# Delta-rule heads of a hybrid encoder block: decays taken with ScalarE's bias, norms on transposed tiles, two-step doubling levels, and another order of the lanes

## The chip, the cores and the metric

The kernel runs on one core of a Trainium2 chip. The core has five engines that run at the same time and wait for each other by semaphores: TensorE (PE in the profile; its weight loads are PEld), VectorE (DVE), ScalarE (ACT), GpSimd (POOL) and SyncE (SP, which here only issues DMAs). PE writes its results to PSUM, which has eight banks of 128 x 512 fp32 values. The metric is the time of one execution on the device, in microseconds (us); lower is better.

## The reference, cut to what matters

A trunk of two layers works on 512 tokens of width 2048 in fp32. The even layer has neighbourhood attention (6 heads), a gated delta rule in both directions (6 heads) and attention to a memory; the odd layer has differential attention (6 heads) and attention to the memory. The change touches the delta rule of the even layer:

```python
q = l2norm(q) * (HEAD_DIM ** -0.5); k = l2norm(k)
G = jnp.cumsum(g, axis=-1)
decay = jnp.exp(jnp.where(lower_incl, G[..., :, None] - G[..., None, :], -jnp.inf))
a_mat = jnp.where(lower_strict, jnp.einsum('bhnid,bhnjd->bhnij', kb, k) * decay, 0.0)
sol = lax.linalg.triangular_solve(a_mat + jnp.eye(C, dtype=f32), rhs, left_side=True, lower=True)
qk = jnp.einsum('bhnid,bhnjd->bhnij', q, k) * decay
q_dec = q * jnp.exp(G)[..., None]

def step(S, xs):
    u_c, w_c, qk_c, qd_c, kd_c, ge = xs
    v_new = u_c - jnp.einsum('bhcd,bhde->bhce', w_c, S)
    o = jnp.einsum('bhcd,bhde->bhce', qd_c, S) + jnp.einsum('bhij,bhje->bhie', qk_c, v_new)
    S = S * ge[..., None, None] + jnp.einsum('bhcd,bhce->bhde', kd_c, v_new)
    return S, o
```

It runs once forwards and once on the flipped tokens, and the two outputs are added and normed.

## The kernel before

Most of the work is GEMMs against streamed weights. Each fp32 operand is split into a high part that PE can take in one pass (`wh`, `hi`, by an ACT copy) and the rest (`wl`, `lo`, by a DVE subtraction), and each product is the sum of three passes, `hi*wh + hi*wl + lo*wh`. Products of 128 x 128 in the delta rule and all transposes are done in plain fp32.

The order on PE is written by hand. A GEMM is a generator (`chunk`, `group`) that yields after about 350 columns or more, and at each yield `Lanes.step` runs (line 222): it goes over five queues of side work and advances the front task of each by one step, up to that task's next `yield`, if a small clock kept during the build says that what the last step made is ready by now. A step puts its instructions at the end of the queue of each engine that it uses; every engine takes its queue in order. The lanes are: 0 the recurrence (`dn_rec`, and `dn_finish`, which norms the sum of both directions), 1 attention (`na_task`, memory and differential attention), 2 preparation (`dn_prep`), 3 convolution taps (`dn_taps`), 4 the doubling levels (`dn_levels`). When attention's head h+1 is projected (`na_head`), its GEMM of 384 columns holds four PSUM banks, one for each 128 tokens; each delta head in recurrence holds one more (`oacc`). All side work takes what is left: `pb()` (line 291) hands out a bank, and PE's first write into it waits until the last reader of the tile that was there has finished. The build's clock does not know of banks.

For each of the six delta heads `dn_prep` (line 973) does the following, in steps. It loads a row of cumulated gates G, broadcast over 128 partitions, for both directions (`g_d`). It transposes k (`tr4`: four 128 x 128 transposes into one bank), squares the result on ACT, sums on DVE, takes `x^-0.5` on POOL (`rsqrt`), and scales k on DVE straight from that bank (`b.kt`). It transposes v, sums the squares of q by four products with a column of ones, transposes the scaled k back, and makes k k^T and k^T q for four chunks of 128 tokens. Then for each direction it makes the decays: for each chunk DVE subtracts a gate column and takes a maximum or minimum with a mask of +-1e30 (`mx_`, `mn_`), one instruction for 128 x 128, ACT takes the exponential of all 512 columns, and POOL multiplies by k k^T (this is `A`), by k^T q (`qk`) and, for `qd`, exp(G) by q. A goes to DRAM in both directions, comes back as 16 x 16 blocks (`a_d`), DVE solves those with 15 short multiplications and 15 reductions, and the result goes through DRAM again (`x_d`) and is loaded as the start `N` of the inverse.

`dn_levels` (line 1078) doubles the block size three times (16, 32, 64) for each direction: a copy of the needed halves to dense tiles on ACT (`dense`), a product (`pps`), a transpose (`mps`), two evacuations (`Mm` on ACT, `Pm` on DVE, with a mask), a second product (`nps`), and a subtraction into `N` on DVE. Each level has three yields and takes three banks.

After the sixth head come the 16 gate GEMMs (`gates`), which multiply each head's finished output by its gate, and the output projection.

Of the kernel before, what the change touches and what calls it, by code (L numbers as in the profile page):

```python
# [10 lines left out]
AF = mybir.ActivationFunctionType  # L11
# [3 lines left out]
P = 128  # L15
# [196 lines left out]
class Lanes:  # L212
# [8 lines left out]

    def step(self):
        c = self.clock
        for q in self.q:
            if q:
                for e in list(q[0]):
                    if e[1] + LAG > c.t["pe"]:
                        continue
                    c.due = 0.0
                    if next(e[0], None) is None:  # L230
                        q[0].remove(e)
                    e[1] = c.due
                if not q[0]:
                    q.pop(0)
# [17 lines left out]
def tile_hybrid(ctx: ExitStack, tc: tile.TileContext, xT, memT, we, wo, wek, wok, weo, woo, vecs, rows, rpb,  # L252
# [576 lines left out]

    g_d = dram.tile([NH * T], F32, name="g_d")  # L830

    def delta_gates():
        load_ba()
        yield 1
# [31 lines left out]
        vec.tensor_copy(G[:, :, 0:6], gv[:, 0, :, 0:6])  # L866
        vec.tensor_copy(G[:, :, 6:12], gv[:, 1, :, 6:12])
        vec.tensor_tensor(sG, G, lnb, op=ALU.add)
        vec.tensor_tensor(ekd, gv[:, 2], G, op=ALU.subtract)
        act(ege, gv[:, 2], AF.Exp)  # L870
        act(ekd, ekd, AF.Exp)
# [101 lines left out]
    def dn_prep(b):  # L973
# [5 lines left out]
            dma(r, bass.AP(tensor=g_d.tensor, offset=g_d.offset + (d * 6 + b.h) * T, ap=[[0, P], [1, T]]))  # L979
            rows_.append(r)  # L980
        b.q, b.k, b.v = b.qkv
        sq = w2()
        act(sq, b.q, AF.Square)
        kps = tr4(b.k)
        sk = w2()
        act(sk, kps, AF.Square)
        ks = small(4)
        vec.tensor_reduce(ks, v3(sk, 4), AX.X, ALU.add)
        vec.tensor_scalar(ks, ks, EPS, None, op0=ALU.add)
        rk = small(4)  # L990
        rsqrt(rk, ks)
# [3 lines left out]
        vps = tr4(b.v)  # L995
        b.vt = w2()
        copy(b.vt, vps)
        qs = pb()
        for t in range(TT):
            mm(qs[:, t:t + 1], sq[:, t * P:(t + 1) * P], ones[:, 0:1], start=True, stop=True)  # L1000
        rq = small(4)
        vec.tensor_scalar(rq, qs[:, 0:4], EPS, None, op0=ALU.add)
        b.rq = small(4)
        rsqrt(b.rq, rq)
        vec.tensor_scalar(b.rq, b.rq, SCALE, None, op0=ALU.mult)
# [13 lines left out]
        for d in range(2):  # L1019
            hd, n = d * 6 + b.h, "fb"[d]  # L1020
            R = rows_[d]
            A = w2()
            for t in range(TT):
                s = slice(t * P, (t + 1) * P)
                vec.scalar_tensor_tensor(A[:, s], R[:, s], sG[:, t, hd:hd + 1], C("mx_" + n), op0=ALU.subtract,
                                         op1=ALU.max)
            act(A, A, AF.Exp, scale=-1.0)
            pool_e.tensor_tensor(A, A, kk, op=ALU.mult)
            b.a.append(A)
            qk = w2()  # L1030
            for t in range(TT):
                s = slice(t * P, (t + 1) * P)
                vec.scalar_tensor_tensor(qk[:, s], R[:, s], G[:, t, hd:hd + 1], C("mn_" + n), op0=ALU.subtract,
                                         op1=ALU.min)
            act(qk, qk, AF.Exp)
            qd = w2()
            act(qd, R, AF.Exp)
            yield 1
            if d == 0:
                At[0] = A  # L1040
            else:
                aps = tr4(A)
                At[1] = w2()
                copy(At[1], aps)
                yield 1
            dma(rows_ap(ad, d), v3(At[d], 4))
            pool_e.tensor_tensor(qk, qk, kq, op=ALU.mult)
            pool_e.tensor_tensor(qd, qd, b.q, op=ALU.mult)
            b.qk.append(qk)
            b.qd.append(qd)  # L1050
# [27 lines left out]
    def dn_levels(b, d):  # L1078


        while len(b.a) <= d:
            yield 1
        A = b.a[d]

# [4 lines left out]
            copy(o.rearrange("p (k s) -> p k s", s=s), half(a, s, 1))  # L1089
            return o  # L1090

        Ad = []
        at = w2()
        Ad.append(dense(A, 16, at[:, 0:256]))
        yield 1
        Ad.append(dense(A, 32, at[:, 256:512]))
        Ad.append(dense(A, 64, w2()[:, 0:256]))
        while b.inv is None:
            yield 1
        N = b.inv[d]  # L1100
        for li, s in enumerate((16, 32, 64)):
            Nd = dense(N, s, w2()[:, 0:256])
            pps = pb()
            for i in range(2):
                c = slice(i * P, (i + 1) * P)
                mm(pps[:, c], Ad[li][:, c], half(N[:, i * 2 * P:(i + 1) * 2 * P], s, 0), start=True, stop=True)
            yield 1
            mps = pb()
            for i in range(2):
                c = slice(i * P, (i + 1) * P)  # L1110
                transpose(mps[:, c], Nd[:, c])
            Mm = w2()
            copy(Mm[:, 0:256], mps[:, 0:256])
            Pm = w2()
            vec.tensor_tensor(v3(Pm[:, 0:256], 2), v3(pps[:, 0:256], 2),
                              lv[:, li, :].unsqueeze(1).to_broadcast([P, 2, P]), op=ALU.mult)
            yield 1
            nps = pb()
            for i in range(2):
                c = slice(i * P, (i + 1) * P)  # L1120
                mm(nps[:, c], Mm[:, c], Pm[:, c], start=True, stop=True)
            vec.tensor_tensor(half(N, s, 0), half(N, s, 0), nps[:, 0:256].rearrange("p (k s) -> p k s", s=s),
                              op=ALU.subtract)
            yield 1
        b.n[d] = N

    def dn_rec(b, d, hd):
# [456 lines left out]
```

## Time and profile before

| | |
|---|---|
| median of 3 runs | 2004.64 us (2000.44 to 2007.24) |
| the profiled execution | 2001.6 us, of which the span from the first to the last instruction is 1999.8 us |
| busy in the span | PE 98%, PE weight loads 84%, DVE 57%, ACT 39%, POOL 7% |
| granted PE clock, mean | 0.996 of full speed |

The share of PE is of time in which a matmul is on its way; what it waits for, and the clock that it is granted, are in other views. In rows of the trace an instruction stands as line, engine, operation and `out<-in` by the program's tile names without their numbers: `pa` is a PSUM bank, `w` a working tile of 128 x 512, `ct` the constants (an identity, among others, so `pa<-ct,w` on line 335 is a transpose), `s` a small column. Nearly all DVE, ACT and POOL instructions are recorded under the helper's line 207.

### The profile page before, as it was taken

The page shows a single profiled execution, that of the slowest core. Times are in us where ns is not written, and L with a number is a line of the kernel's source. Part 1 is how long each engine was busy: PE and PEld are TensorE (multiplying, and loading weights), DVE is VectorE, ACT ScalarE, POOL GpSimd, SP SyncE. Part 2 cuts the span into 40 slices and gives each one's busy share as a digit, 9 for nine tenths or more (in the row PEclk, how much of TensorE's full clock was granted, in tenths as well). Part 3 has the DMA queues.
Part 4 walks back from the last instruction along what each step waited for, and adds up shares of the span by engine and source line. Part 5 has one row for each costly group of instructions (what it writes and reads, how often), then busy time and mean ns, then how long its engine had stood idle before and what let it go on. Part 6 is the DMA issues. An engine that isn't in the chain of part 4 may idle for free.

```text
span 1999.8 us, 25600 instructions
## 1 busy us (share of the span) xinstructions
PE 1966.4 (98%) x9907; PEld 1684.4 (84%) x9907; DVE 1138.8 (57%) x2150; ACT 774.8 (39%) x1388; POOL 138.2 (7%) x127
## 2 busy tenths in 40 slices
PE   9999999999998999999999999999999999999999
PEld 7988899888888788888888888888888888888887
DVE  6676666757576675656334456566556557435322
ACT  5655344444444434334224343434434333324111
POOL 0100020202020202000000000001001010000000
PEclk9999999999999999999999999999999999999999
DMA  6555433323323233324444423222222323333442
GB/s 217 158 166 168 138 99 102 87 85 87 101 81 98 75 117 112 111 91 128 144 151 128 132 85 95 73 97 74 85 95 74 95 76 114 98 113 122 142 142 90
DMA packets 101050, 222.28 MB, mean 111 GB/s; under 512 B 22288, under 2 KB 36928, under 8 KB 100928
## 3 DMA queue, kind: packets, MB, share of 16 engines
q1 hardware_dynamic: 71232, 207.45, 32.9%
q10 hardware_dynamic: 29696, 13.19, 2.5%
q8 instruction: 78, 1.28, 0.3%
q14 instruction: 44, 0.36, 0.1%
HBM read 199.96 MB, written 20.65 MB: 110 GB/s over the span
## 4 chain that ended last, share of the span: by engine, by line
PE 91%; DVE 3%; issue 2%; ACT 1%; DMA 1%; POOL 1%; ACTq 0%; SPq 0%; POOLq 0%; DVEq 0%
PE pa L265 88%; PE pa L335 4%; DVE w L207 2%; ACT w L207 1%; POOL w L207 1%; DVE wl L207 1%; DMA w<-x_d 1%; POOL s L207 0%; DVE s L207 0%; ACT wh L207 0%; DMA w<-in_xT_dram 0%; DMA w<-in_lvl_dram 0%; DVE vn L207 0%; DVE vb L207 0%; ACTq L342 0%
## 5 line engine op out<-in xcount | busy, mean ns | idle before, releaser
L207 ACT ACTIVATE wh<-wr 128x1024 fp32r<-128x1024 f32 (+3 forms) x333 | 341.8, 1027 | 703.1 <-PE pa L265 551.6
L207 DVE TENSOR_TENSOR wl<-wr,wh 128x1024 fp32r<-128x1024 f32 (+3 forms) x333 | 397.6, 1195 | 362.7 <-ACT wh L207 361.7
L265 PE MATMUL pa<-hi,wh 128*128 128x512 f32 x1312 | 519.0, 396 | 0.0
L265 PE MATMUL pa<-hi,wl 128*128 128x512 f32 x1312 | 511.8, 390 | 0.0
L265 PE MATMUL pa<-lo,wh 128*128 128x512 f32 x1312 | 511.5, 390 | 0.0
L265 PE MATMUL pa<-wh,hi 128*128 128x512 f32 (+2 forms) x1088 | 416.3, 383 | 1.3 <-ACT wh L207 1.3
L265 PE MATMUL pa<-wl,hi 128*128 128x512 f32 (+2 forms) x1088 | 405.9, 373 | 0.4 <-DVE wl L207 0.4
L265 PE MATMUL pa<-wh,lo 128*128 128x512 f32 (+2 forms) x1088 | 405.5, 373 | 0.0
L265 PEld LDWEIGHTS pa<-hi,wl 128*128 128x128 f32 x1312 | 246.6, 188 | 52.2
L265 PEld LDWEIGHTS pa<-lo,wh 128*128 128x128 f32 x1312 | 247.1, 188 | 48.4
L265 PEld LDWEIGHTS pa<-hi,wh 128*128 128x128 f32 x1312 | 247.0, 188 | 48.2
L265 PEld LDWEIGHTS pa<-wh,hi 128*128 128x128 f32 x1088 | 205.9, 189 | 28.4 <-ACT wh L207 2.3
L265 PEld LDWEIGHTS pa<-wh,lo 128*128 128x128 f32 x1088 | 205.6, 189 | 28.0
L265 PEld LDWEIGHTS pa<-wl,hi 128*128 128x128 f32 x1088 | 206.2, 190 | 26.6 <-DVE wl L207 0.7
L207 ACT ACTIVATE w<-pa 128x512 f32<-128x512 f32 (+3 forms) x222 | 111.1, 524 | 177.4 <-PE pa L335 98.5
L207 ACT ACTIVATE w<-w 128x512 f32<-128x512 f32 (+4 forms) x285 | 141.9, 536 | 84.6 <-DVE w L207 64.4
L265 PE MATMUL pa<-w,w 128*128 128x256 f32 (+3 forms) x1128 | 167.7, 293 | 4.6 <-DMA w<-x_d 1.9
L265 PEld LDWEIGHTS pa<-w,w 128*128 128x128 f32 (+1 forms) x1128 | 151.5, 188 | 15.7 <-DVE w L207 3.9
L207 POOL TENSOR_TENSOR s<-s,mhalf 128x1 f32<-128x1 f32 (+3 forms) x58 | 75.3, 1299 | 1200.1 <-DVE s L207 1197.1
L207 DVE TENSOR_TENSOR w<-pa,w 128x512 fp32r<-128x512 f32 (+2 forms) x108 | 71.2, 680 | 137.3 <-PE pa L265 108.1
L207 ACT ACTIVATE w<-pa,s 128x256 f32<-128x256 f32 (+1 forms) x104 | 58.7, 570 | 136.6 <-DVE s L207 102.1
L335 PE MATMUL pa<-ct,w 128*128 128x128 f32 (+1 forms) x640 | 92.2, 273 | 8.8 <-ACT w L207 4.2
(151 smaller groups left out, 1437.0 us busy)
## 6 DMA issues: line engine op xcount, KB each, us to landing
wr<-in_wo_dram SPq DMA_DIRECT2D x112, 512.0 KB, 3.6
wr<-in_we_dram SPq DMA_DIRECT2D x75, 512.0 KB, 3.6
wr<-in_weo_dram SPq DMA_DIRECT2D x32, 512.0 KB, 3.6
wr<-in_woo_dram SPq DMA_DIRECT2D x32, 512.0 KB, 3.5
wr<-in_we_dram SPq DMA_DIRECT2D x40, 384.0 KB, 3.1
w<-in_xT_dram SPq DMA_DIRECT2D x32, 256.0 KB, 4.6
wr<-in_wek_dram SPq DMA_DIRECT2D x16, 512.0 KB, 4.3
wr<-in_wok_dram SPq DMA_DIRECT2D x16, 512.0 KB, 3.8
```

The lines of the kernel that those rows point to most:

```text
L207: return f(*a, **k)
L265: nc.tensor.matmul(o, lhsT, rhs, start=start, stop=stop)
L335: nc.tensor.transpose(o, i, ident if idn is None else idn)
```

## The change

Six edits, all in the build of the side work.

- `Lanes.step` goes over the lanes in the order 0, 2, 3, 4, 1: attention's task steps after the others.
- The norms of k and q: k's squares are summed by ACT itself (`accum_out`), in four instructions of 128 columns instead of one of 512 and a DVE reduction. q is transposed too (`tr4(b.q)`, one more bank) and treated in the same way, and the products of its squares with a column of ones go.
- The decays: DVE takes the maximum and the minimum of the row G and the mask once, over 512 columns; the gate column enters as ACT's bias, so ACT does four exponentials of 128 columns where it did one of 512. A tile `gg` now holds -G for that.
- The products with k k^T and k^T q go from POOL to DVE; the one for `qd` stays on POOL. `dn_prep` has two more yields in each direction.
- `dn_levels` waits for the start of the inverse before it copies anything from A; `pps` and `mps` are halves of one bank and are written in one step, `Mm` and `Pm` lie in one tile, the dense copy of N for the next level is made behind the subtraction, and a level has two yields.
- One DVE instruction for -G, once.

```diff
-        for q in self.q:
+        for q in self.q[:1] + self.q[2:] + self.q[1:2]:
...
+        vec.tensor_scalar(gg, G, -1.0, None, op0=ALU.mult)
+        nG.append(gg)
...
-        sq = w2()
-        act(sq, b.q, AF.Square)
         kps = tr4(b.k)
         sk = w2()
-        act(sk, kps, AF.Square)
         ks = small(4)
-        vec.tensor_reduce(ks, v3(sk, 4), AX.X, ALU.add)
+        for t in range(TT):
+            c = slice(t * P, (t + 1) * P)
+            act(sk[:, c], kps[:, c], AF.Square, accum_out=ks[:, t:t + 1])
...
-        qs = pb()
+        qps = tr4(b.q)
+        rq = small(4)
         for t in range(TT):
-            mm(qs[:, t:t + 1], sq[:, t * P:(t + 1) * P], ones[:, 0:1], start=True, stop=True)
-        rq = small(4)
-        vec.tensor_scalar(rq, qs[:, 0:4], EPS, None, op0=ALU.add)
+            c = slice(t * P, (t + 1) * P)
+            act(sk[:, c], qps[:, c], AF.Square, accum_out=rq[:, t:t + 1])
+        vec.tensor_scalar(rq, rq, EPS, None, op0=ALU.add)
...
-            A = w2()
+            A, qk, qd = w2(), w2(), w2()
+            vec.tensor_tensor(v3(A, 4), v3(R, 4), cm(C("mx_" + n)), op=ALU.max)
+            vec.tensor_tensor(v3(qk, 4), v3(R, 4), cm(C("mn_" + n)), op=ALU.min)
             for t in range(TT):
                 s = slice(t * P, (t + 1) * P)
-                vec.scalar_tensor_tensor(A[:, s], R[:, s], sG[:, t, hd:hd + 1], C("mx_" + n), op0=ALU.subtract,
-                                         op1=ALU.max)
-            act(A, A, AF.Exp, scale=-1.0)
-            pool_e.tensor_tensor(A, A, kk, op=ALU.mult)
+                act(A[:, s], A[:, s], AF.Exp, bias=sG[:, t, hd:hd + 1], scale=-1.0)
+            vec.tensor_tensor(A, A, kk, op=ALU.mult)
             b.a.append(A)
-            qk = w2()
+            yield 1
             for t in range(TT):
                 s = slice(t * P, (t + 1) * P)
-                vec.scalar_tensor_tensor(qk[:, s], R[:, s], G[:, t, hd:hd + 1], C("mn_" + n), op0=ALU.subtract,
-                                         op1=ALU.min)
-            act(qk, qk, AF.Exp)
-            qd = w2()
+                act(qk[:, s], qk[:, s], AF.Exp, bias=nG[0][:, t, hd:hd + 1])
             act(qd, R, AF.Exp)
...
-            pool_e.tensor_tensor(qk, qk, kq, op=ALU.mult)
+            vec.tensor_tensor(qk, qk, kq, op=ALU.mult)
+            yield 1
...
     def dn_levels(b, d):
-        while len(b.a) <= d:
+        while b.inv is None:
             yield 1
...
+        both = w2()
+        Ad = [dense(A, 16, both[:, 0:256])]
+        Nd = dense(N, 16, both[:, 256:512])
         for li, s in enumerate((16, 32, 64)):
-            Nd = dense(N, s, w2()[:, 0:256])
+            yield 1
             pps = pb()
...
-            yield 1
-            mps = pb()
+            mps = pps[:, 256:512]
...
+            if li == 0:
+                both = w2()
+                Ad += [dense(A, 32, both[:, 0:256]), dense(A, 64, both[:, 256:512])]
             yield 1
             nps = pb()
...
-            yield 1
+            if li < 2:
+                Nd = dense(N, 2 * s, w2()[:, 0:256])
+        yield 1
```

How this moves instructions is seen best in the built order of an engine's queue. In the rows below a tile carries its number; `pa_5102` is the 5102nd tile of the build, `ct_79` the constants, `wh`, `wl`, `hi`, `lo` the split operands of a GEMM.

First place: PE before the change, in the first doubling level of the third head (head 2), while attention's head 3 is projected. The two transposes for each direction are rows 3 and 4; their products `pps` (tiles 5075 and 5080) stand nine GEMM products ahead.

```order
L265 MATMUL pa_5027<-wl_4991,hi_191 128x384
L265 MATMUL pa_5027<-wh_4990,lo_192 128x384
L335 MATMUL pa_5102<-ct_79,w2_5073 128x128 x2
L335 MATMUL pa_5109<-ct_79,w2_5078 128x128 x2
L265 MATMUL pa_5028<-wh_4990,hi_191 128x384
L265 MATMUL pa_5028<-wl_4991,hi_191 128x384
```

In the build's table of banks tile 5109 lies in the bank of tile 5102, so between the last write to the one and the first to the other there is no other work on PE.

The same place on PE after the change:

```order
L265 MATMUL pa_4905<-wh_5174,lo_389 128x384
L265 MATMUL pa_5265<-w2_5170,w2_5237 128x128 x2
L335 MATMUL pa_5265<-ct_79,w2_5237 128x128 x2
L265 MATMUL pa_5276<-w2_5172,w2_5240 128x128 x2
L335 MATMUL pa_5276<-ct_79,w2_5240 128x128 x2
L265 MATMUL pa_4906<-wh_5174,hi_388 128x384
```

Product and transposes of a direction now stand together in one bank, and the two directions lie in banks whose earlier tiles PE left long before.

Second place: PE before the change where the k of the fifth head (head 4) is transposed for its norm (tile 6398).

```order
L335 MATMUL pa_6398<-ct_79,w2_6170 128x128 x4
L265 MATMUL pa_6019<-wh_6206,hi_363 128x384
L265 MATMUL pa_6019<-wl_6207,hi_363 128x384
L265 MATMUL pa_6019<-wh_6206,lo_364 128x384
L265 MATMUL pa_6415<-vb_6376,w2_6083 128x128
L265 MATMUL pa_6421<-S_6380,w2_5491 128x128
```

Tile 6421, a product of the recurrence, lies in the bank of 6398, three GEMM products and one fp32 product later.

And after the change, with k in tile 6263:

```order
L335 MATMUL pa_6263<-ct_79,w2_5919 128x128 x4
L265 MATMUL pa_6279<-w2_6191,w2_6250 128x128 x2
L335 MATMUL pa_6279<-ct_79,w2_6250 128x128 x2
L265 MATMUL pa_6290<-w2_6193,w2_6253 128x128 x2
L335 MATMUL pa_6290<-ct_79,w2_6253 128x128 x2
L265 MATMUL pa_5882<-wh_6173,hi_432 128x384
```

Here tile 6290, of the levels of head 3, lies in the bank of 6263, with the products and transposes of tile 6279 between; for the third head, whose k norm stood as closely before, the next tile in that bank now comes some 30 rows later.

Third place: DVE before the change where the decays of the fourth head (head 3), backwards direction, are made (`w2_5590` is A, `w2_5597` is qk, `vb` and `vn` belong to the recurrence).

```order
L207 SCALAR_TENSOR_TENSOR S_5563<-S_5464,ege_99,pa_5561 128x128
L207 SCALAR_TENSOR_TENSOR w2_5590<-w2_5401,sG_96,ct_79 128x128 x4
L207 SCALAR_TENSOR_TENSOR w2_5597<-w2_5401,G_95,ct_79 128x128 x4
L207 TENSOR_TENSOR wl_5579<-wr_5315,wh_5578 128x1024
L207 SCALAR_TENSOR_TENSOR vb_5566<-pa_5616,nekb_97,vb_5566 128x128
L207 COPY w2_5635<-pa_5028 128x256
```

After the change, the forward direction of that head (`w2_5514` is A, `w2_5515` is qk, `w2_5486` and `w2_5493` are k k^T and k^T q):

```order
L207 TENSOR_TENSOR w2_5514<-w2_5323,ct_79 128x512
L207 TENSOR_TENSOR w2_5508<-pa_5503,lv_2029 128x256
L207 TENSOR_TENSOR w2_5515<-w2_5323,ct_79 128x512
L207 TENSOR_TENSOR w2_5514<-w2_5514,w2_5486 128x512
L207 TENSOR_TENSOR wl_5528<-wr_5253,wh_5527 128x1024
L207 TENSOR_TENSOR w2_5170<-w2_5170,pa_5539 128x4x64
L207 TENSOR_TENSOR w2_5172<-w2_5172,pa_5543 128x4x64
L207 TENSOR_TENSOR w2_5515<-w2_5515,w2_5493 128x512
```

Eight instructions of 128 columns have become four of 512, two of which came from POOL; the one that multiplies A waits for ACT's exponentials, and the next weight split (`wl`) and the levels' subtractions stand behind it.

## Rows read from the trace of the kernel before

**Rows 1.** The page, busy time: us, share of the span, instructions.

```profile
PE 1966.4 (98%) x9907; PEld 1684.4 (84%) x9907; DVE 1138.8 (57%) x2150; ACT 774.8 (39%) x1388; POOL 138.2 (7%) x127
```

**Rows 2.** Busy time by stretch: the delta rule; a stretch of GEMM alone (columns named).

```profile
core 0: us, PE busy (x) PEld busy (x) DVE busy (x) ACT busy (x) POOL busy (x), PEclk, DMA share, GB/s
250.00:850.00 600.00, 575.48 (x3282) 514.89 (x3281) 399.47 (x904) 252.69 (x527) 84.03 (x68) 0.99 0.33 96
...
950.00:1000.00 50.00, 50.00 (x222) 41.42 (x221) 16.20 (x17) 11.62 (x13) 0.00 (x0) 1.00 0.46 144
```

**Rows 3.** What PE waited for, 250 to 850 us: total us, times, longest us.

```profile
PE pa L265 <- DVE w L207: 9.1, 4, 3.4
PE pa L335 <- ACT w L207: 4.2, 8, 0.7
PE pa L265 <- DVE vn L207: 3.5, 6, 0.9
PE pa L335 <- DVE w L207: 2.0, 1, 2.0
PE pa L265 <- DMA w<-x_d: 1.9, 2, 1.2
PE pa L335 <- DVE vn L207: 1.4, 1, 1.4
PE pa L265 <- DVE vb L207: 0.7, 1, 0.7
PE pa L335 <- DVE vb L207: 0.6, 1, 0.6
PE pa L335 <- DVE s L207: 0.5, 2, 0.3
```

**Rows 4.** Timeline at the levels of head 2: start us, us, what [idle before].

```profile
513.26 0.36 ACT L207 ACTIVATE w<-pa 128x256 f32<-128x256 f32 x1
513.68 0.44 PE L335 MATMUL pa<-ct,w 128*128 128x128 f32 x2 [0.52 <-ACT w L207]
```

**Rows 5.** Timeline at the k norms of head 2 and head 4.

```profile
434.66 0.60 ACT L207 ACTIVATE w<-pa 128x512 f32<-128x512 f32 x1 [1.61 <-PE pa L335]
436.26 1.01 POOL L207 TENSOR_TENSOR s<-s,mhalf 128x4 f32<-128x4 f32 x1 [61.93 <-DVE s L207]
437.30 0.69 DVE L207 TENSOR_TENSOR w<-pa,s 128x512 f32<-128x512 f32 x1 [1.12 <-POOL s L207]
438.14 0.46 PE L265 MATMUL pa<-vb,w 128*128 128x128 f32 x2 [2.31 <-DVE w L207]
...
643.38 0.60 PE L335 MATMUL pa<-ct,w 128*128 128x128 f32 x4
647.50 1.19 PE L265 MATMUL pa<-S,w 128*128 128x128 f32 x4 [2.77 <-DVE w L207]
```

**Rows 6.** Timeline of DVE and PE while POOL multiplies for head 4.

```profile
663.67 3.99 DVE L207 SCALAR_TENSOR_TENSOR w<-w,sG,ct 128x128 f32<-128x128 f32 x4
672.89 0.46 PE L265 MATMUL pa<-vd,w 128*128 128x128 f32 x2 [3.41 <-DVE w L207]
```

**Rows 7.** Busy time and clock just behind long waits (columns as in rows 2).

```profile
401.60:405.00 3.40, 3.40 (x10) 2.64 (x10) 2.41 (x4) 1.61 (x3) 0.00 (x0) 0.50 0.56 179
647.30:650.70 3.40, 3.20 (x11) 3.23 (x12) 1.64 (x4) 0.00 (x0) 0.00 (x0) 0.51 0.28 55
672.90:676.30 3.40, 3.40 (x17) 2.90 (x18) 1.47 (x6) 1.53 (x6) 0.38 (x1) 1.00 0.50 154
```

**Rows 8.** Groups by line and shape, 250 to 850 us (DVE, POOL, ACT, PE): count | busy us, mean ns.

```profile
L207 DVE SCALAR_TENSOR_TENSOR w<-w,sG,ct 128x128 f32<-128x128 f32 x48 | 24.9, 572 | 0.0
L207 DVE SCALAR_TENSOR_TENSOR w<-w,G,ct 128x128 f32<-128x128 f32 x48 | 19.7, 460 | 0.0
L207 DVE SCALAR_TENSOR_TENSOR w<-w,w 128x512 f32<-128x512 f32 x24 | 16.5, 687 | 7.6 <-ACT w L207 7.5
L207 POOL TENSOR_TENSOR w<-w,w 128x512 f32<-128x512 f32 x36 | 53.8, 1519 | 40.2 <-ACT w L207 33.7 <-PE pa L265 6.5
L207 ACT ACTIVATE w<-w 128x512 f32<-128x512 f32 x65 | 39.6, 625 | 23.3 <-DVE w L207 23.1
L207 ACT ACTIVATE vb<-w,bet 128x128 f32<-128x128 f32 x44 | 16.6, 394 | 0.0
L265 PE MATMUL pa<-ct,w 128*128 128x1 f32 x48 | 5.8, 242 | 0.2 <-DVE vn L207 0.2
```

More of the change, by code (lines that the diff above doesn't have):

```diff
@@ L830, in tile_hybrid @@
     g_d = dram.tile([NH * T], F32, name="g_d")
+    nG = []
     def delta_gates():
@@ L1090, in dense @@
             return o
-        Ad = []
-        at = w2()
-        Ad.append(dense(A, 16, at[:, 0:256]))
-        yield 1
-        Ad.append(dense(A, 32, at[:, 256:512]))
-        Ad.append(dense(A, 64, w2()[:, 0:256]))
-        while b.inv is None:
+        N = b.inv[d]
+        both = w2()
+        Ad = [dense(A, 16, both[:, 0:256])]
+        Nd = dense(N, 16, both[:, 256:512])
+        for li, s in enumerate((16, 32, 64)):
             yield 1
-        N = b.inv[d]
-        for li, s in enumerate((16, 32, 64)):
-            Nd = dense(N, s, w2()[:, 0:256])
             pps = pb()
@@ L1111, in dn_levels @@
                 transpose(mps[:, c], Nd[:, c])
[L1112 to L1115, printed above, removed]
+            both = w2()
+            Mm, Pm = both[:, 0:256], both[:, 256:512]
+            copy(Mm, mps)
+            vec.tensor_tensor(v3(Pm, 2), v3(pps[:, 0:256], 2),
                               lv[:, li, :].unsqueeze(1).to_broadcast([P, 2, P]), op=ALU.mult)
+            if li == 0:
+                both = w2()
+                Ad += [dense(A, 32, both[:, 0:256]), dense(A, 64, both[:, 256:512])]
             yield 1
@@ L1123, in dn_levels @@
                               op=ALU.subtract)
-            yield 1
+            if li < 2:
+                Nd = dense(N, 2 * s, w2()[:, 0:256])
+        yield 1
         b.n[d] = N
```

## Prediction

> **What bounds the kernel now.** I read the page's busy times first, then busy time by stretch, then what PE waited for, and last the timeline around the longest waits. PE is busy 98% of the span [rows 1], so nothing but PE's own work, its waits and its clock can move the time. In a stretch of GEMM alone PE has no idle time at all: 222 products in 50.00 us, 0.225 us each [rows 2]; by columns one of 384 takes about 0.17 us. Where the delta rule runs, 250 to 850 us, PE is busy 575.48 of 600 us: 24.5 us idle [rows 2]. The rest of the page's 33 us of idle time lies at the start, in the short stretches before 250 us and behind PE's last instruction, and the change hardly touches it. So 24.5 us, plus what the clock loses there, is nearly all that there is to win.
>
> The waits in that stretch sum to 23.9 us [rows 3]. What PE waits for there is mostly not an operand but a bank. At 513 us two transposes go into a bank that ACT must first empty of the two before them: its copy takes 0.36 us, and PE stands 0.52 us [rows 4]. At 438 and 647 us the bank is that of the transposed k: ACT squares it (from 434.66), DVE sums, POOL takes the power (1.01 us), and only when DVE has scaled it (ends 437.99) may PE write there; PE stood 2.31 and 2.77 us [rows 5]. The names fit: the released products take `vb` or `S`, which nobody was late with, yet the releaser is DVE's `w`. I followed this through the built order, counting the PE work (at the prices above) between the last write to a tile and the first write to the next in its bank. From 250 to 850 us 23 banks are taken again within 0.8 us, nine of them with nothing between.
>
> Three long waits have another cause or a second price. At 672.89 PE stood 3.41 us for a bank of attention's GEMM that DVE had not evacuated, because DVE was slowed while POOL multiplied: four instructions of 128 columns took 3.99 us [rows 6]. And behind the waits at 400.6, 438.1 and 647.5 the granted clock fell to 0.50 (1.2 GHz in place of 2.4) for 3.4 us each; behind that at 672.9 it stayed at 1.00 [rows 7]. A stretch of 3.4 us at half clock costs 1.7 us, three cost 5.1.
>
> **The change, term by term**, against the profiled execution's 2001.6 us.
>
> *PE's work.* 24 products with a column of ones go; the trace has 48 records of them, 5.8 us busy [rows 8], in six runs of eight, so about (5.8/6 - 0.24)/7 = 0.10 us from one record to the next. 24 transposes come, at (0.60 - 0.27)/3 = 0.11 us each from a run of four that takes 0.60 us [rows 5], the last one's tail of 0.27 taken off as an estimate. 48 x 0.10 - 24 x 0.11 = 2.2 us less. All other PE instructions stay.
>
> *Banks.* A level takes two banks in place of three, its transposes have PE's products in front of them in the same bank, and attention's step, which holds two or three banks, stands behind the others. In the order after, one bank is taken again within 0.8 us where there were 23, none with nothing between: that of head 4's k (0.67 us). From rows 3 I put down to such banks: of ACT `w` 3.6 of 4.2 us (seven of the eight waits), of DVE `w` 5.7 of 9.1 (all but the 3.41), DVE `vn` before transposes 1.4, `vb` 0.7 and 0.6, `s` 0.5: 12.5 us [rows 3]. What stays is head 4's. Its chain before is 434.66 to 437.99, 3.3 us [rows 5]; with four squares of 128 columns at about 0.39 each (nearest row 394 ns) in place of one of 0.60 and a reduction of about 0.69, it is 3.5 or so, less the 0.67 us of cover: 3.0 us. Term: -9.5 us; bounds -12.5 and, if banks collide in new places, -4.
>
> *POOL and DVE.* 24 of POOL's 36 multiplications (1519 ns) go to DVE. DVE loses 96 subtractions (24.9 + 19.7 us) and gains 48 instructions of 512 columns, at 687 ns 33.0 us [rows 8], and loses six reductions: some 15 us less work for DVE in all. That the same instruction takes 572 ns in one group and 460 in the other, and 1000 each in rows 6, shows it is POOL that stretches them. The 3.41 us wait should mostly go: -2.5, bounds 0 and -3.4 [rows 3].
>
> *The inverse's DMA.* PE waited 1.9 us for it [rows 3]. Before, 3.1 to 9.9 us of PE work lie between the issue of that load and its first product; after, 7.2 to 15.7, since the levels make their dense copies first. Term -1.9, bounds 0 and -1.9. The copies on ACT now wait for the load instead; what is queued behind them there is the next weight copy, for which PE has three units in hand.
>
> *Attention's 2.0 us* at 400.6, behind the sixteen-row solve on DVE [rows 3]: its step now stands behind the others'. -1, bounds 0 and -2.
>
> *Clock.* Three stretches before [rows 7], one or two after: -2.6, bounds 0 and -5.1.
>
> *New waits.* ACT does 96 exponentials with a bias in place of 24 (394 for 128 columns, 625 for 512 [rows 8]: up to 24 x (4 x 0.394 - 0.625) = 22.8 us more) and 48 squares in place of 12, some 11 us more: up to 34 us on an engine that is busy 252.69 of 600 [rows 2]. DVE's `Pm` now waits for ACT's `Mm`, as both read one bank, and A's product waits for four exponentials; behind each stand a weight split, the levels' subtractions and the recurrence's `vn`. Nearest row: PE's waits for `vn`, 3.5 us in all [rows 3]. Bounds 0 and 9 us; I take 3, nearer to that row, since DVE has less to do and no POOL against it.
>
> Sum: -2.2 - 9.5 - 2.5 - 1.9 - 1.0 - 2.6 + 3.0 = -16.7, so 1984.9 us for the profiled execution. That one was 3.0 us below the median of the runs shown, so 1988 for the median. All bounds at their best: -27 (1977); at their worst: -4 - 2 + 9 = +3 (2008).
>
> Against the change speaks what small pieces cost on ACT. The rows say 394 ns for 128 columns with a column operand, and 625 for 512 without [rows 8]: four pieces take 2.5 times as long as one, 22.8 us more for the 24 sets of decays. If all of that fell on the path that PE waits for, the sum would be -16.7 - 3 + 22.8, so no gain (2008); I hold it off, as ACT is idle for 347 of the 600 us [rows 2] and PE's long waits name POOL, DVE and banks. It is the mechanism of the slower rival below. The Trainium skill, page "ScalarE: Activation LUTs", section "What ACT_TABLE_LOAD costs", has it as a rule: about 280 ns plus 0.833 ns per column with a column as bias, 186 plus the same without, and 93 ns of overlap between neighbours. By it a set of decays would take an estimated 4 x 387 - 3 x 93 - 612 = 0.66 us more, 24 of them 16 us, and the sum with all of it on the path would be 2001; the trace bears out the 387 and the 612, and no row of before shows the overlap.
>
> **The rivals.**
>
> *The waits move.* The delta heads take as many steps, PE's order shifts everywhere, and new waits of the same kind come where the count of PE work sees none, since it knows nothing of queues. For it: at 672.9 and 400.6 us PE waited with more than 4 us of work between. Against it: banks taken again within 2 us fall from 81 to 33. Then half of the banks' 9.5, the clock's 2.6 and all of 2.5 + 1.9 + 1.0 come back: about 1999.
>
> *Slower: ACT's small pieces hold DVE.* Each of 12 directions ends its first step with DVE's product waiting for four exponentials; if a weight copy (about 1 us) stands ahead, DVE stands 2 to 3 us, and an evacuation of attention's GEMM behind it makes PE wait, as at 672.9. It decides from 16.7/12 = 1.4 us of new PE wait per direction. At 2.5 us each, with the clock dropping in half of them (6 x 1.7): +40 - 17 = 2028. For it: DVE is PE's releaser in most of rows 3. Against it: PE waits for DVE `vn`, the recurrence's own link, only six times.
>
> *The chain gets too long.* A head's preparation has more yields, and from the gates' load to A's second store head 1 now takes 48 us of PE work, not 30. Head 5's last product moves from 816 to 834 us of PE work, and its gate comes at 875: 40 us are left, so this costs nothing until a head is later by that. If it did, the ending would run with nothing beside it, some 10 us more than forecast, 1998.
>
> *More than forecast.* No clock drop stays and `vn` goes too: 1974 to 1977.
>
> **How the numbers follow.** Forecast 0.70 (own range 1979 to 1996), waits move 0.14 (1995 to 2004), slower by ACT and DVE 0.07, too long a chain 0.03, more 0.06. The predicted time is 1988. From 1977 to 2001 lie the forecast, most of the first rival and the third; outside are the slower case, the upper end of the first and the best case's half: under 0.2. A measurement of this kernel tells 0.3%, about 6 us, from no change. Faster by more (under 1998.6): 0.70 + 0.06 + a good half of the first rival's 0.14 + 0.02 = 0.86. Within: 0.07. Slower: 0.07.
>
> **What would show it.** In the profile after: PE idle from 250 to 850 us at about 10 us in place of 24.5; hardly a wait of PE's transposes for ACT `w`; one long wait for DVE `w` near the k norm of head 4; POOL near 47 us in that stretch, and DVE's 512-column products near 0.69 us; `PE <- DMA x_d` gone; ACT 25 to 35 us busier. The prediction is wrong if PE's waits for DVE or ACT come back under other names with the same sum, or if the clock falls as often as before.

## The result, and the profile after

| | before | after |
|---|---|---|
| median | 2003.6 us (4 runs, 2000.44 to 2007.24) | 1971.01 us (4 runs, 1969.3 to 1973.51) |
| profiled execution, its span | 2001.6, 1999.8 us | 1970.47, 1968.7 us |

The ratio is 0.9838, 95% interval 0.9817 to 0.9858: 32.5 us faster (28 to 37), where 17 were forecast, and below the range's lower end. The page's busy times and span after:

```profile
span 1968.7 us, 25599 instructions
PE 1952.4 (99%) x9883; PEld 1677.4 (85%) x9883; DVE 1117.8 (57%) x2097; ACT 792.4 (40%) x1544; POOL 97.8 (5%) x103
```

Busy time from 250 to 850 us, columns as in [rows 2], and PE's waits there, as in [rows 3]:

```profile
250.00:850.00 600.00, 592.93 (x3416) 534.97 (x3414) 394.49 (x873) 281.10 (x699) 43.89 (x44) 1.00 0.34 101
```

```profile
PE pa L335 <- DVE w L207: 4.1, 2, 2.5
PE pa L265 <- issue: 2.7, 1, 2.7
```

PE is idle 7.07 us there, not 24.5; three waits are left of 26. The transposes' waits for ACT `w`, the waits for `vn` and `vb` and that for the inverse's DMA are gone. The one named "issue" is the k norm of head 4, as [rows 5] show it for before; by the built order it is a bank again, that of the transposed k:

```profile
620.36 0.60 PE L335 MATMUL pa<-ct,w 128*128 128x128 f32 x4
622.49 1.01 POOL L207 TENSOR_TENSOR s<-s,mhalf 128x4 f32<-128x4 f32 x1 [53.65 <-DVE s L207]
623.53 0.69 DVE L207 TENSOR_TENSOR w<-pa,s 128x512 f32<-128x512 f32 x1 [1.19 <-POOL s L207]
624.32 0.68 PE L265 MATMUL pa<-w,w 128*128 128x128 f32 x4 [2.69 <-issue]
```

The first longer wait is not new. It is the wait of 2.0 us that [rows 3] show (at 400.6 us), now in another head: attention's softmax divides on DVE only after a chain of exponentials on ACT, and PE's transposes wait for that. Before, and then after:

```profile
399.88 0.19 DVE L207 RECIPROCAL s<-s 128x5 f32<-128x5 f32 x1 [1.44 <-ACT w L207]
400.11 1.26 DVE L207 TENSOR_SCALAR w<-w,s 128x256 f32<-128x256 f32 x5
400.61 1.16 PE L335 MATMUL pa<-ct,w 128*128 128x128 f32 x8 [2.00 <-DVE w L207]
...
309.26 0.19 DVE L207 RECIPROCAL s<-s 128x5 f32<-128x5 f32 x1 [1.56 <-ACT w L207]
309.49 1.26 DVE L207 TENSOR_SCALAR w<-w,s 128x256 f32<-128x256 f32 x5
309.99 1.14 PE L335 MATMUL pa<-ct,w 128*128 128x128 f32 x8 [2.47 <-DVE w L207]
```

The third (1.61 us, at 516.1) is for DVE's last product in `dn_finish`, which PE transposes.

The groups by shape from 250 to 850 us, as in [rows 8]. ACT's pieces for the decays cost 31.1 us where 24 wide ones of 625 ns cost 15:

```profile
L207 ACT ACTIVATE w<-w,sG 128x128 f32<-128x128 f32 x48 | 15.4, 390 | 4.8 <-DVE w L207 4.8
L207 ACT ACTIVATE w<-w,gg 128x128 f32<-128x128 f32 x48 | 15.7, 391 | 0.0
L207 DVE TENSOR_TENSOR w<-w,w 128x512 f32<-128x512 f32 x36 | 27.4, 766 | 4.3 <-ACT w L207 3.7
L207 POOL TENSOR_TENSOR w<-w,w 128x512 f32<-128x512 f32 x12 | 16.4, 1365 | 114.8 <-ACT w L207 114.8
```

Where the span's 31.1 us went: PE's idle time over the whole span fell from 1999.8 - 1966.4 = 33.4 to 1968.7 - 1952.4 = 16.3 us (17.1). The three stretches at half clock [rows 7] are gone (an estimated 5.1). PE's own work is some 2.2 less, as forecast; this was not measured apart. And a wait costs PE more than its idle time shows: products that start 0.23 us apart are drawn 0.39 us long (a timeline of PE after), so by estimate each of the 23 waits that are gone gave back 0.16 us more, 3.7 in all. About 3 us stay unassigned.

```profile
306.68 0.39 PE L265 MATMUL pa<-hi,wh 128*128 128x512 f32 x1
306.91 0.39 PE L265 MATMUL pa<-lo,wh 128*128 128x512 f32 x1
```

### The profile page after: what moved, and what is told of

The parts are those of the page before. It is cut to its first block, busy times and chain, and to the rows that moved or that the text cites. A ratio compares the mean times of both kernels' runs of the same rounds, so it can differ in the third digit from the quotient of the medians.

```text
span 1968.7 us, 25599 instructions
## 1 busy us (share of the span) xinstructions
PE 1952.4 (99%) x9883; PEld 1677.4 (85%) x9883; DVE 1117.8 (57%) x2097; ACT 792.4 (40%) x1544; POOL 97.8 (5%) x103
## 4 chain that ended last, share of the span: by engine, by line
PE 95%; DVE 2%; ACT 1%; issue 1%; DMA 0%; POOL 0%; SPq 0%; ACTq 0%; DVEq 0%
PE pa L265 92%; PE pa L335 4%; DVE w L207 2%; DVE wl L207 1%; ACT w L207 0%; DMA w<-in_xT_dram 0%; ACT wh L207 0%; DMA ba<-ba_d 0%; POOL s L207 0%; DVE s L207 0%; ACT hi L207 0%; DVE du L207 0%; DVE vn L207 0%; SPq L118 0%; DVE gg L207 0%
## 5 line engine op out<-in xcount | busy, mean ns | idle before, releaser
L207 DVE TENSOR_TENSOR wl<-wr,wh 128x1024 fp32r<-128x1024 f32 (+3 forms) x333 | 392.9, 1181 | 369.7 <-ACT wh L207 368.7
L265 PE MATMUL pa<-wh,hi 128*128 128x512 f32 (+2 forms) x1088 | 410.7, 377 | 1.7 <-ACT wh L207 1.7
L207 ACT ACTIVATE w<-pa 128x512 f32<-128x512 f32 (+4 forms) x264 | 119.6, 480 | 137.0 <-PE pa L335 68.6
L207 ACT ACTIVATE w<-w 128x512 f32<-128x512 f32 (+4 forms) x255 | 124.0, 529 | 73.8 <-DVE w L207 58.8
L265 PE MATMUL pa<-w,w 128*128 128x256 f32 (+4 forms) x984 | 150.2, 296 | 3.5 <-issue 2.7
L265 PEld LDWEIGHTS pa<-w,w 128*128 128x128 f32 (+1 forms) x984 | 133.3, 188 | 13.1 <-issue 2.9
L335 PE MATMUL pa<-ct,w 128*128 128x128 f32 x664 | 94.5, 272 | 4.1 <-DVE w L207 4.1
```

The lines of the kernel that those rows point to most:

```text
L207: return f(*a, **k)
L265: nc.tensor.matmul(o, lhsT, rhs, start=start, stop=stop)
L335: nc.tensor.transpose(o, i, ident if idn is None else idn)
```

## Experiments

That the mechanism held and the sum was half of the gain asked for the other half. Theory 1 is the prediction's: PE's waits for banks were most of what there was, and the new levels bring it. Theory 2: POOL's 24 multiplications held DVE, and so PE, at far more places than the one that I priced. Theory 3: the order of the lanes did it. All kernels compute the whole reference. "us" is (ratio - 1) x 2004; an interval is about 3 us to either side. The idle time is PE's from 250 to 850 us in the profiled execution (24.5 before, 7.1 after).

| run | what it is | median | ratio (95%) | us | PE idle |
|---|---|---|---|---|---|
| in_levels | before, with the new levels | 1993.35 | 0.9949 (0.9936-0.9961) | -10 | 18.9 |
| in_norm | before, with the new norms | 1992.35 | 0.9939 (0.9927-0.9952) | -12 | 18.9 |
| before_dve | before, the two products on DVE | 1989.67 | 0.9919 (0.9904-0.9935) | -16 | 16.6 |
| levels_dve | before, new levels and products on DVE | 1979.23 | 0.9873 (0.9858-0.9888) | -25 | 8.7 |
| in_levels_decay | before, new levels and decays | 1975.84 | 0.9856 (0.9843-0.987) | -29 | 6.4 |
| out_levels | after, old levels | 1982.54 | 0.9891 (0.9878-0.9905) | -22 | 12.8 |
| out_decay | after, old decays (POOL too) | 1985.93 | 0.9908 (0.9895-0.9922) | -18 | 16.7 |
| out_order | after, old lane order | 1972.64 | 0.9838 (0.9821-0.9856) | -32 | 5.1 |
| out_norm | after, old norms | 1968.51 | 0.9818 (0.9801-0.9834) | -36 | 1.8 |
| after_twobanks | after, `mps` in its own bank | 1971.38 | 0.983 (0.9813-0.9847) | -34 | 5.0 |
| after_kold | after, old k norm, new q norm | 1972.95 | 0.984 (0.9825-0.9854) | -32 | 5.4 |
| after_pool | after, the two products on POOL | 1979.11 | 0.9872 (0.9855-0.9889) | -26 | 11.8 |
| after_nopool | after, all three products on DVE | 1968.63 | 0.9821 (0.9807-0.9836) | -36 | 4.0 |
| after_sub | after, old subtractions and wide exponentials | 1967.64 | 0.9816 (0.9803-0.983) | -37 | 3.6 |
| sub_oldnorm | after_sub, old norms | 1970.57 | 0.9835 (0.982-0.9849) | -33 | 4.1 |
| sub_nopool | after_sub, all three products on DVE | 1966.83 | 0.9813 (0.9799-0.9827) | -37 | 3.0 |
| sub_nopool_same_chip | the same, beside the next | 1966.93 | 0.9811 (0.9797-0.9826) | -38 | 3.0 |
| after_control | the changed kernel again | 1973.28 | 0.984 (0.9824-0.9855) | -32 | 7.0 |

An edit here changes more than its own instructions. The small clock kept during the build gives a product of 512 columns 75 + 1.05 x 512 = 613 ns on DVE and 150 + 2.2 x 512 = 1276 ns on POOL (lines 256 and 257), so moving two products moves steps too: of PE's 9907 matmuls some 2100 stand in another place in the trace of before_dve than in that of before. In after_pool it is some 2000 of 9883 against after, in after_control none. So what an edit does by its own mechanism has to be read from the waits, beside the time.

**The levels, put in and taken out.** The edit is the `dn_levels` part of the diff, in either direction.

> The kernel before with the new doubling levels alone (one bank for product and transposes, two steps a level). Theory 1 (PSUM banks taken again too early made PE wait): in the built order the banks taken again within 0.8 us of PE work fall from 23 to 7 between 250 and 880 us, so most of the gain is here: 1980 to 1988 us. Theory 2 (POOL and DVE slowing each other and late evacuations made PE wait; the decays cure it): 1998 to 2004 us, no measurable change. The 3.41 us wait behind POOL's products stays under both.

> The changed kernel with the old doubling levels (three banks and three steps a level). Theory 1: banks taken again within 0.8 us rise from 1 to 15, some 0.5 us each and clock drops behind the longer waits: 1979 to 1988 us. Theory 2: 1970 to 1974 us, since DVE and POOL are as relieved as in the changed kernel.

Put in they brought 10 us; without them 22 of 32.5 us are left, so they are worth 11. Both answers are near the bank term of 9.5, though that held other banks too. out_levels lies in theory 1's range; in_levels lies in neither, since theory 1 had nearly the whole forecast gain in the levels. The waits bear the mechanism out: PE's transposes wait for ACT `w` 8 times in before, 9 in before_dve and 11 in in_norm, and never in in_levels, levels_dve and in_levels_decay. Yet PE waited under other names (in_levels, 250 to 850 us):

```profile
PE pa L335 <- DVE w L207: 7.0, 3, 5.2
PE pa L265 <- DVE vb L207: 5.1, 5, 2.6
PE pa L265 <- DVE vn L207: 5.0, 4, 1.8
```

8.3 us of the last two rows stand behind POOL's products (below). Whether `mps` lies in the bank of `pps` or in its own doesn't matter:

```diff
-            mps = pps[:, 256:512]
+            mps = pb()[:, 0:256]
```

> The changed kernel with the transposes of a level in a bank of their own again, steps as changed. Theory 1: 365 banks taken in place of 329, but only 3 within 0.8 us against 1, since the second bank is asked for right behind the first: 1971 to 1976 us; if sharing the bank itself is what counts, 1980 us or more. DVE no longer waits for ACT's copy of the same bank.

**Norms and order.** The norms as in the diff, in and out; the old order of the lanes, `for q in self.q:`; and the old k norm alone.

> The kernel before with the new norms alone. Both theories: PE's work falls by 2.2 us, the tight banks only from 23 to 20; 1998 to 2003 us, hardly measurable.

> The changed kernel with the old norms. Theory 1: 2.2 us of PE work come back and 3 tight banks stand against 1: 1973 to 1977 us. Theory 2 and 3 say the same, 1971 to 1975 us.

> The changed kernel with the old order of the lanes (attention second). Theory 1: banks taken again within 0.8 us are 0 against 1, within 2 us 24 against 33, so no loss: 1968 to 1974 us. Theory 3 (attention's step behind the others is what keeps PE from waiting): 1980 us or more.

> The changed kernel with k's old norm (one square of 512 columns on ACT and DVE's sum) and q's new one. Theory A: 0 tight banks; the wait of 2.7 us for k's bank at head 4 goes, since another tile comes into it, and PE keeps the 2.2 us that q's new norm saves: 1965 to 1969 us, below the changed kernel. If that wait only moves, 1970 to 1972 us.

The norms brought 12 us to the old kernel and nothing, or a small loss, to the new one; both times lie below the ranges given. They shift the order of everything behind them. In in_norm PE's waits for DVE `w`, 11.1 us in five before, are down to 0.5 in two, while others grew:

```profile
PE pa L335 <- ACT w L207: 6.9, 11, 1.0
PE pa L265 <- DMA w<-x_d: 5.1, 3, 3.1
```

So another order alone can be worth 12 us to the old kernel. That these are the waits that the other edits remove anyway is likely, and not shown. The old k norm with the new q norm left the time as it was, a little above both ranges: the wait for k's bank is gone, as theory A had it, but in the profiled execution the clock fell to 0.50 for 6.8 us behind the softmax's wait, where in the changed kernel's it did not. The order of the lanes does nothing once the rest is in; theory 3 falls. (The kernel in_levels_decay differs from out_norm by that order alone, and there the old order was 7 us slower: without the new norms it counts.) The new order on the old kernel, and the new decays on it, were not tried.

**The decays and POOL.** The old decays put back whole, and then the two lines alone, in both kernels:

```diff
-            pool_e.tensor_tensor(A, A, kk, op=ALU.mult)
+            vec.tensor_tensor(A, A, kk, op=ALU.mult)
...
-            pool_e.tensor_tensor(qk, qk, kq, op=ALU.mult)
+            vec.tensor_tensor(qk, qk, kq, op=ALU.mult)
```

> The changed kernel with the old decays (DVE subtractions of 128 columns, products on POOL). Theory 1: tight banks rise from 1 to 7, and evacuations late behind POOL cost the 2 to 4 us of the old 3.41 us wait: 1974 to 1980 us. Theory 2: most of the gain is lost, 1988 us or more.

> The changed kernel with the products by k k^T and k^T q back on POOL, all else as changed. Theory 1: tight banks as in the changed kernel (1), DVE slowed again by POOL: 1971 to 1976 us. Theory 2: POOL's products slow DVE and its evacuations, and waits of 2 to 4 us come back, several of them with clock drops: 1980 to 1990 us.

> The kernel before with one thing changed: the products by k k^T and k^T q on DVE instead of POOL. Theory A (POOL's products hold DVE, and DVE's late evacuations make PE wait): the 8 us that POOL costs in the changed kernel come off here too, 1993 to 1998 us, and four DVE subtractions never take 4 us. Theory B (the wide maximum and the bias are what counts in the decays): 2001 to 2006 us. Theory C (any new arrangement moves the long waits away by chance): 1990 to 2000 us, but with DVE's own durations unchanged.

> The kernel before with the new levels and the new decays, without the new norms and the new order of the lanes. Theory A: both causes are gone, 2 tight banks are left, 1968 to 1974 us. Theory C: with other places for the same work some long waits come back, 1975 to 1985 us.

> The kernel before with the new levels, and with the products by k k^T and k^T q on DVE; old subtractions, exponentials, norms and lanes. If banks and POOL are the two causes and add up: 11 + 14 us less, 1976 to 1981 us. If the order of steps (the new yields, the lanes) is a third cause of like size: 1983 us or more.

These two lines, in the kernel before, brought 16 us (13 to 19); put back into the changed kernel they cost 7, and the old decays put back whole cost 14. Levels and lines together give 25 us, as 10 + 16 let expect. The other ranges were missed: before_dve lies below all three, after_pool just below theory 2's, out_decay between the two, and in_levels_decay in theory C's instead of A's. That POOL holds DVE is plain, though. For the subtractions of [rows 6], 3.99 us for four there, the timeline of before_dve has these rows; POOL is silent at the first and the last:

```profile
650.45 1.13 DVE L207 SCALAR_TENSOR_TENSOR w<-w,sG,ct 128x128 f32<-128x128 f32 x4
658.58 1.56 POOL L207 TENSOR_TENSOR w<-w,w 128x512 f32<-128x512 f32 x1 [5.35 <-ACT w L207]
659.16 1.12 DVE L207 SCALAR_TENSOR_TENSOR w<-w,sG,ct 128x128 f32<-128x128 f32 x1
660.21 1.13 DVE L207 SCALAR_TENSOR_TENSOR w<-w,G,ct 128x128 f32<-128x128 f32 x4
```

Four subtractions take 1.13 us when POOL is silent; beside one of its products a single one takes 1.12. How the delay reaches PE is seen in after_pool's timeline:

```profile
559.26 1.28 ACT L207 ACTIVATE w<-w,sG 128x128 f32<-128x128 f32 x4 [5.67 <-DVE w L207]
559.69 4.94 DVE L207 SCALAR_TENSOR_TENSOR w<-pad,cw,w 128x512 f32<-128x512 f32 x4
560.62 3.47 POOL L207 TENSOR_TENSOR w<-w,w 128x512 f32<-128x512 f32 x2 [6.99 <-ACT w L207]
564.41 1.36 POOL L207 TENSOR_TENSOR w<-w,w 128x512 f32<-128x512 f32 x1 [0.32 <-ACT w L207]
564.56 0.74 DVE L207 SCALAR_TENSOR_TENSOR w<-pa,vt,w 128x512 fp32r<-128x512 f32 x1
565.22 1.63 DVE L207 TENSOR_TENSOR wl<-wr,wh 128x1024 fp32r<-128x1024 f32 x1
566.77 0.74 DVE L207 SCALAR_TENSOR_TENSOR w<-pa,vt,w 128x512 fp32r<-128x512 f32 x1
567.56 0.66 PE L265 MATMUL pa<-w,w 128*128 128x256 f32 x3 [2.67 <-DVE w L207]
```

Four convolution taps take 4.94 us beside two of POOL's products, at 748 ns each where nothing disturbs them (the group after: 60 of them, 44.9 us). Behind them in DVE's queue stand a weight split (1.63 us, mean 1.22) and the evacuation that PE waits for: 2.67 us for a `w` that has nothing to do with the decays. The first evacuation, which reads one operand from PSUM, takes its usual 0.74 us beside POOL. The Trainium skill, page "SBUF — State Buffer", section "Who interferes with whom", has this as a rule: a DVE instruction with two SBUF inputs contends with a GpSimd instruction that reads SBUF, by an exclusive lock, and one with at most one SBUF input, outside DVE's two-port modes, does not. The rows agree in both.

In out_decay the same delay falls on the recurrence's link `vb` (timelines of DVE, POOL and PE):

```profile
753.52 3.17 DVE L207 SCALAR_TENSOR_TENSOR w<-w,sG,ct 128x128 f32<-128x128 f32 x4
756.87 0.60 DVE L207 SCALAR_TENSOR_TENSOR vb<-pa,nekb,vb 128x128 f32<-128x128 f32 x2
```

```profile
753.55 2.72 POOL L207 TENSOR_TENSOR w<-w,w 128x512 f32<-128x512 f32 x2 [1.42 <-ACT w L207]
```

```profile
757.27 0.75 PE L265 MATMUL pa<-vb,w 128*128 128x128 f32 x4 [2.41 <-DVE vb L207]
```

PE's wait is recorded for `vb`, and no POOL row is near it in the list of waits.

How much of PE's waiting is this? I take the waits in front of which DVE was busy without a gap since one of its instructions was held beside a product of POOL. In after and in levels_dve there are none. In after_pool there are two, 1.28 us (at 464.13) and the 2.67, and behind the second the clock is at 0.50 for 3.4 us, an estimated 1.7 more: 5.7 of the 7 us. In out_decay they are five, 6.1 us, and a sixth of 3.52 us (at 566.98) came through ACT: an exponential waited 4.61 us for DVE's late subtraction, and the copy of the recurrence's state stands behind it in ACT's queue. Around that one the clock is at 0.50 for 6.8 us, an estimated 3.4 at most: 13 of the 14. The clock's rows, after_pool's and then out_decay's (columns as in [rows 2]):

```profile
568.00:571.40 3.40, 3.40 (x17) 3.11 (x16) 1.68 (x11) 2.19 (x8) 0.39 (x1) 0.50 0.29 105
...
565.50:572.30 6.80, 5.32 (x21) 4.94 (x22) 3.40 (x5) 3.02 (x8) 3.28 (x3) 0.50 0.23 78
```

In in_levels, the kernel before without the old levels' waits, they are six, 8.3 of 18.9 us, all for `vb` and `vn`. The longest:

```profile
450.25 3.83 POOL L207 TENSOR_TENSOR w<-w,w 128x512 f32<-128x512 f32 x3 [4.96 <-issue]
450.33 3.90 DVE L207 SCALAR_TENSOR_TENSOR w<-w,sG,ct 128x128 f32<-128x128 f32 x3
454.55 0.49 PE L265 MATMUL pa<-vb,w 128*128 128x128 f32 x2 [2.55 <-DVE vb L207]
```

In the kernel before there are only two, 0.65 us (at 454.97) and the 3.41: 4.1 of 24 us. Its waits at 400.61, 438.14 and 647.50, 7.1 us with the three stretches at half clock behind them, come 36 us or more after POOL's last product of decays (the rows with `w`; `s` is the norm's power):

```profile
359.89 3.97 POOL L207 TENSOR_TENSOR w<-w,w 128x512 f32<-128x512 f32 x3 [1.42 <-ACT w L207]
436.26 1.01 POOL L207 TENSOR_TENSOR s<-s,mhalf 128x4 f32<-128x4 f32 x1 [61.93 <-DVE s L207]
...
564.58 4.97 POOL L207 TENSOR_TENSOR w<-w,w 128x512 f32<-128x512 f32 x3 [1.42 <-ACT w L207]
645.62 1.01 POOL L207 TENSOR_TENSOR s<-s,mhalf 128x4 f32<-128x4 f32 x1 [65.07 <-DVE s L207]
```

So theory 2 stands, beside the banks: with the levels in, the two lines bring 15 us more (in_levels to levels_dve), and those six waits are gone. What is not shown is that POOL itself cost the kernel before 16 us. In before_dve the steps stand elsewhere: the waits at 400.61 and 438.14 are gone, the k norm of head 4 still waits (2.78 us), and one of 2.06 us has come. Its profiled execution has 7.9 us less idle time in PE and is 9.9 us shorter, not 16. How much of that is the other order (theory C) stays open; a run that moves the products and keeps PE's order was not made.

**The bias, and the rest of POOL.** The old subtractions and one wide exponential, with the products on DVE and the new yields; then the third product on DVE too (`vec.tensor_tensor(qd, qd, b.q, op=ALU.mult)`); then both, and the old norms:

```diff
-            vec.tensor_tensor(v3(A, 4), v3(R, 4), cm(C("mx_" + n)), op=ALU.max)
...
-                act(A[:, s], A[:, s], AF.Exp, bias=sG[:, t, hd:hd + 1], scale=-1.0)
+                vec.scalar_tensor_tensor(A[:, s], R[:, s], sG[:, t, hd:hd + 1], C("mx_" + n), op0=ALU.subtract,
+                                         op1=ALU.max)
...
+            act(A, A, AF.Exp, scale=-1.0)
```

> The changed kernel with the old subtractions of 128 columns on DVE and the old exponentials of 512 on ACT; the products stay on DVE. Theory A: without POOL in its way DVE does the subtractions in 0.28 us each, 24 x (8 x 0.28 - 2 x 0.69) = 21 us more DVE work, hidden: 1970 to 1975 us. Theory B: the other 7 us of the decays' part come back, 1977 to 1981 us.

> The changed kernel with the last product (exp(G) by q) on DVE too, so POOL keeps only the short powers. If every product of POOL costs PE time in proportion (8 us for 24): 4 us less, 1965 to 1969 us. If only products on the way to A's chain cost: 1970 to 1973 us.

> The changed kernel without the wide maximum and bias and without the new norms: order of lanes, new levels, new yields, products on DVE. If both parts cost on their own (3.4 and 2.5 us): 1963 to 1967 us; PE's work is 2.7 us more than with the new norms. If they only hid the same wait: 1967 to 1971 us.

> The changed kernel without the wide maximum and bias, and with all three products on DVE. Fewest close banks of all (9 within 2 us) and no long POOL work: 1963 to 1967 us, the best of the runs; no wait of PE over 1 us from 250 to 850 us.

> The changed kernel itself, beside the next one on the same chip: 1969 to 1974 us.

> The changed kernel without the wide maximum and bias and with all three products on DVE, beside the changed kernel on the same chip: 3 to 5 us below it if the difference between the two chips was not the cause, equal if it was.

The change's namesake, the bias, brings nothing: without it the kernel is 3 to 4 us faster by the medians, though the intervals overlap; that is below both ranges. Only with POOL multiplying do the subtractions seem to cost: out_decay is 7 us slower than after_pool (it also has the old yields, and another order). The third product on DVE (after_nopool) lies in the range for a cost in proportion, but its interval overlaps the changed kernel's. The old norms, a gain in out_norm, cost 3 us here: effects of this size don't add. The best kernel is sub_nopool. On the chip that ran it beside the changed kernel it took 1966.93 us (1966.66 to 1967.26) against 1973.28 (1970.34 to 1974.66). Its waits of PE from 250 to 850 us, none over a microsecond:

```profile
PE pa L265 <- ACT vd L207: 0.9, 1, 0.9
PE pa L265 <- DVE vn L207: 0.9, 2, 0.4
PE pa L265 <- DVE w L207: 0.4, 1, 0.4
PE pa L265 <- ACT w L207: 0.3, 1, 0.3
```

## Why the prediction was off, point by point

- **PE's work** (-2.2): the counts are as forecast (24 records fewer in sum); not measured apart.
- **Banks** (-9.5): about right in size. The waits that it names are gone, and the k norm of head 4 stayed, at 2.69 us where 3.0 were forecast. That the levels are worth 10 to 11 us from either side fits, but is another sum, with some of the clock in it.
- **POOL and DVE** (-2.5, at most -3.4): the step that failed, by its size. I priced it from "the 3.41 us wait" alone, the one place where the list of waits and the timeline showed POOL together. Measured: the two lines put back into the changed kernel cost 7 us, twice the bound, and the old decays whole 14, and the waits behind DVE's delay make up most of both. With only the levels new, such waits are 8.3 us, where the kernel before shows 4.1: I priced POOL by a trace in which PE waited mostly for other things. (The 16 us in the old kernel are of the same lines, mixed with another order.) The hint was in [rows 8], and I quoted it: the same subtraction took 572 ns in one group and 460 in the other (414 and 465 in before_dve, where one product in three is still POOL's). I read it as DVE time, 15 us that DVE has to spare, and not as a delay of what stands behind on DVE.
- **Terms that were not there**: PE's waits for `vn` (3.5 us) I left standing as the recurrence's own, at nothing, and none is left. What a wait costs beside its idle time, an estimated 3.7 us for all, was in no term either. In sum, for the profiled executions: idle time fell by 17.1 us where the terms for waits make 11.9, the clock gave 5.1 and not 2.6, those 3.7 come on top, and about 3 us stay unassigned; that is the 14.4 us between 16.7 and 31.1.
- **The inverse's DMA** (-1.9) and **attention's 2.0 us** (-1): the first is gone. The second was not cured but moved: the same step of the softmax waits 2.47 us in another head, again just behind a sixteen-row solve.
- **Clock** (-2.6, at most -5.1): its best case, in the profiled execution. It is not a fixed gain (below).
- **New waits** (+3, at most 9): ACT got 28.4 us busier (281.10 - 252.69), as said, and PE has no wait that names it. DVE's products stand at 766 ns in a group of 36, of which they are 24, and at 683 in sub_nopool's group of 48; 0.69 was forecast.
- **Against the change**, the small pieces on ACT. Four take 1.28 us (the row at 559.26), so 0.66 us more than one of 0.625, and the Trainium skill's rule ("ScalarE: Activation LUTs", "What ACT_TABLE_LOAD costs") gave 0.66; the groups of after say 31.1 - 15 = 16 us in all, which is its 16 too. The slower rival fell since DVE had room: no `w` of a decay holds an evacuation for long. What remains of the cost is at most the 3 to 4 us that after_sub is faster.
- **The rivals**: "waits move" happened for the softmax's alone, and its sum did not come back. "The chain gets too long" cost nothing: behind 850 us PE is idle for 3.9 us before and after. "More than forecast" came true as far as no clock drop and no wait for `vn` were left, at a chance of 0.06, and 1971 is below its range too. What it names are symptoms; POOL is one cause behind them.

Of the 32.5 us, the levels and the two product lines bring 25 when both are put in; taken out one at a time they cost 11 and 7. The other 7 are what norms, order, bias and yields make together, and no one of them has it: each put in or taken out alone shows between +4 and -12, by what else is in the kernel. That share stays open.

## What to carry to other kernels

When an engine's instructions have two durations in one profile, find who runs beside the long ones, and price the delay of everything that stands behind them in that queue, under whatever name PE waits for it; a list of waits names only the last link. Test such a suspicion with the smallest edit, here two lines moved to another engine, and then look in the waits whether the edit moved anything else: where a build orders the instructions by its own estimates, it does, and a run's time alone does not tell the cause. And take parts out of the new kernel as well as putting them into the old: here the same norms were worth 12 us in one and nothing in the other.

## What the runs showed of the hardware

- A POOL product of 1.3 to 1.8 us holds a DVE instruction with two SBUF operands nearly to its own end, and not one whose first operand is in PSUM (rows of after_pool and before_dve); 24 such products cost the changed kernel 7 us. One instruction with a single SBUF tensor and a column was held too (TENSOR_SCALAR `w<-pad,cw` in after, at 468.13): 1.40 us, beside a product from 467.95 to 469.24, where its group's mean is 0.54.
- The clock behind the same wait falls in one execution and not in another of the same program. Busy time and granted clock (columns as in rows 2) behind the wait at 310 us, in after and then in after_control:

```profile
310.00:313.40 3.40, 3.40 (x18) 2.73 (x19) 3.28 (x8) 2.35 (x6) 0.00 (x0) 1.00 0.58 170
```

```profile
307.00:310.90 3.90, 1.45 (x7) 1.14 (x6) 2.30 (x12) 3.03 (x11) 0.00 (x0) 0.78 0.47 116
310.90:314.30 3.40, 3.40 (x10) 2.57 (x10) 2.08 (x4) 2.20 (x6) 0.00 (x0) 0.50 0.83 241
314.30:317.70 3.40, 3.40 (x13) 2.71 (x12) 0.00 (x0) 0.00 (x0) 0.00 (x0) 0.74 0.19 73
```

  The first stays at 2.4 GHz (1.00); the other is at 1.2 GHz (0.50) for a while, and once more behind the k norm of head 4 (0.50 from 626.7 to 630.1 us); PE's order is the same, its waits and idle time nearly so, and its span is 1972.7 us to 1968.7. So part of the spread of the runs, and up to 4 us of a comparison of two profiles, is the clock's.
